# A two-layer encoder step on one core: weights of the feed-forward's first units two units ahead in the program, and leftover output blocks in the last projection

## The chip, the cores and the metric

The kernel runs on one core of a Trainium2 chip. The core has a matrix engine (PE), a vector engine (DVE), a scalar engine (ACT) and a general engine (POOL), each with an instruction queue of its own that runs in order, and a queue (SP) that only starts transfers. Transfers between the chip's memory and the core's on-chip memory run on 16 DMA engines. The metric is the device time of one execution, in microseconds, from the first to the last thing that the core does; lower is better.

## The reference

Two layers work on 640 columns: 512 frames of a new stream and 8 running streams of 16 frames. Each layer has a mixer (layer 0) or an attention (layer 1), and behind it a feed-forward part with a causal convolution of width 3 over the up-projected rows:

```
def _conv_ffn(x, prev, w_up, conv_w, w_down):
    z, st = _causal_dwconv(x @ w_up, conv_w, prev)
    gate, up = jnp.split(z, 2, axis=-1)
    return (jax.nn.silu(gate) * up) @ w_down, st
...
        yp, st_p = _conv_ffn(hp, zero_f, w_up[layer], conv_ffn[layer], w_down[layer])
        ys, st_s = _conv_ffn(hs, state_ffn[layer], w_up[layer], conv_ffn[layer], w_down[layer])
        xp = xp + yp
        xs = xs + ys
```

The model width is 1024 (8 blocks of 128) and the inner width is 2816 (22 blocks of 128 for the gate and 22 for the up rows). All is float32. The change touches only the feed-forward part, which is called once in each layer (`Core.ffn`).

## The kernel before

**Numbers as two halves.** Each float32 operand is held as a high part (a rounded copy, `whi` or `sh` or `hh`) and a low part (the rest, `wlo` or `sl` or `hl`), and each product is three matmuls: high by high, high by low, low by high. A matmul has 320 columns, so 640 columns take two.

There are three ways to make the parts of a weight tile of 128x1024 that SP has loaded into a `raw` buffer. `weights` casts on ACT (L94) and subtracts on DVE (L95). `weights_added` casts on ACT (L102), writes the negative of the high part on ACT (L103) and then lets POOL start a second transfer of the same weights that adds into it (L104); this spares DVE. `weights_down` does the same for two blocks of the down projection (L120, L121, L122).

**Feed-forward.** The 22 units (a block of the gate and the block of the up rows that belongs to it) are grouped in parts of 4, 4, 4, 4, 4 and 2 units (`PARTS`). The first four units are *full units*: 8 chunks times 3 products times 2 halves times 2 blocks, 96 matmuls. Their results are taken out of PSUM by `pad_evac` (DVE, L340 and L341), scaled by the norm's `rb`, which is made beside unit 0 from the PE's column sums and copied out of PSUM on ACT (L325, L326). Then come, for every unit, the convolution `conv` (ACT L346, DVE L348 four times), the gate's silu (L495), the product (L498, L499) and a split into high and low parts.

The other 18 are *pair units*. They compute gate and up rows together with 7 products of 12 matmuls each (`pair_blocks`, `product`, L201) instead of 8. For this the activations are recombined once: `forms` (DVE L152 to L159, behind units 0 and 1) and `settle` (ACT L135 and DVE L136), which overwrites the tiles that the full units read and so must wait for the last of unit 3's matmuls on each of them. The weights are recombined for every unit by `pair_weights`: set A (x11, x12) is the gate tile itself, D (x22) half of the up tile, B (s3, s1) and C (s2, s4) are made by additions (L180) in `raw`, and each set is split (ACT L135, DVE L136). PE uses them in the order A, B, C, B, D, C.

**Down projection.** While the units of one part run, the down projection of the part before is computed, two output blocks in each unit (`downs`, 48 matmuls, between the products of `pair_blocks`), and each block is added to the residual `x` (L359). Parts have 4 units, so 8 output blocks fit. The last part has only 2 units: four output blocks of the part before it (blocks 4 to 7) are left over and are done behind its units, one pair of blocks after the other. At the end `project` does the last part's own down projection for all 8 blocks, 2 chunks each, adds each to `x`, and calls the finish: in layer 0 the next norm's `prep` (ACT L281 and L288, DVE L282, POOL L289), in layer 1 the output's transfer. The last block of layer 1 is done in two halves (`last_block`).

**Buffers.** Weight sets share 5 pairs of buffers `whi` and `wlo`, used in turn in the order in which the program asks for them; `raw` has 4. PSUM has two `zx` buffers and one `d` for blocks, and two `aux`. The order of instructions on each engine is not that of the code: a scheduler, which simulates the program, sets it within what the buffers allow.

**Lead of the weights.** Unit j asks for unit j+1's weights after its own matmuls. Units 0 and 1 use `weights`, units 2 and 3 `weights_added`. For the first pair unit `pair_weights` is called in two pieces (it is a generator with two `yield`s): A before `settle`, the rest behind it. In the later pair units A comes first, then the down weights, then B and C.

## Time and profile before

| | us |
|---|---|
| median of 3 timed runs (1525.31 to 1528.93) | 1527.41 |
| the profiled execution, device time | 1525.84 |
| its span in the profile | 1524.0 |
| feed-forward of layer 0, first evacuation to last | 228.7 to 668 |
| feed-forward of layer 1, first evacuation to the end | 1075.2 to 1524 |

In the profile's rows a start is given in microseconds from the start of the span, then the duration, the engine, the line of the kernel, the operation and its tiles, and in brackets how long the engine had been idle before it and what it had waited for. "xN" joins N alike rows. A busy time of a window counts overlapping instructions of one engine once.

### The profile page before, as it was taken

The page shows a single profiled execution, that of the slowest core. Times are in us where ns is not written, and L with a number is a line of the kernel's source. Part 1 is how long each engine was busy: PE and PEld are TensorE (multiplying, and loading weights), DVE is VectorE, ACT ScalarE, POOL GpSimd, SP SyncE. Part 2 cuts the span into 40 slices and gives each one's busy share as a digit, 9 for nine tenths or more (in the row PEclk, how much of TensorE's full clock was granted, in tenths as well). Part 3 has the DMA queues.
Part 4 walks back from the last instruction along what each step waited for, and adds up shares of the span by engine and source line. Part 5 has one row for each costly group of instructions (what it writes and reads, how often), then busy time and mean ns, then how long its engine had stood idle before and what let it go on. Part 6 is the DMA issues. An engine that isn't in the chain of part 4 may idle for free.

```text
span 1524.0 us, 26325 instructions
## 1 busy us (share of the span) xinstructions
PE 1471.2 (97%) x10576; PEld 1418.3 (93%) x10576; DVE 1047.9 (69%) x1805; ACT 736.9 (48%) x1326; POOL 211.1 (14%) x235
## 2 busy tenths in 40 slices
PE   8999997899999999999999999999699999999998
PEld 6999997899999999989988888888699999999998
DVE  6555438777877777586666657668777686868764
ACT  5422325555555555445544445435455555545551
POOL 4100121101010101135101111003111010101010
PEclk9999998999999999999999999999899999999999
DMA  7222203444444444453534333432254454545342
GB/s 269 77 76 67 67 29 82 133 112 115 106 117 101 115 108 114 81 171 130 171 111 145 109 110 103 161 105 73 54 144 98 99 127 99 127 98 127 97 103 81
DMA packets 74249, 168.04 MB, mean 110 GB/s; under 512 B 13760, under 2 KB 22896, under 8 KB 74000
## 3 DMA queue, kind: packets, MB, share of 16 engines
q1 hardware_dynamic: 49392, 133.79, 27.9%
q0 software_dynamic: 12032, 25.17, 10.4%
q10 hardware_dynamic: 12704, 7.41, 1.6%
q8 instruction: 83, 1.36, 0.4%
q14 instruction: 38, 0.31, 0.1%
HBM read 150.58 MB, written 11.54 MB: 106 GB/s over the span
## 4 chain that ended last, share of the span: by engine, by line
PE 90%; DVE 3%; issue 2%; DMA 2%; ACT 2%; SPq 0%; POOL 0%; DVEq 0%; POOLq 0%
PE mm L251 37%; PE zx L201 20%; PE pj L696 11%; PE aux L201 8%; PE pv L772 3%; PE po L251 2%; PE pt L765 1%; DVE hl L282 1%; PE mm L389 1%; DVE wlo L95 1%; DMA wlo<-w_up 1%; PE pt L851 1%; PE sc L758 1%; PE sc L759 1%; PE scs L830 1%
## 5 line engine op out<-in xcount | busy, mean ns | idle before, releaser
L135 ACT CAST sh<-raw 128x1024 fp32r<-128x1024 f32 (+2 forms) x152 | 142.4, 943 | 192.3 <-PE zx L201 105.4
L251 PE MATMUL mm<-sh,wlo 128*128 128x320 f32 x872 | 203.5, 310 | 5.9 <-ACT sn L216 3.1
L251 PE MATMUL mm<-sh,whi 128*128 128x320 f32 x872 | 200.9, 310 | 2.7 <-ACT sh L135 1.7
L251 PE MATMUL mm<-sl,whi 128*128 128x320 f32 x872 | 199.1, 309 | 0.6 <-DVE sl L136 0.6
L136 DVE TENSOR_TENSOR sl<-raw,sh 128x1024 fp32r<-128x1024 f32 (+2 forms) x152 | 165.0, 1091 | 45.2 <-ACT sh L135 31.0
L348 DVE SCALAR_TENSOR_TENSOR t<-zp,cst,t 128x656 f32<-128x656 f32 x184 | 163.6, 896 | 29.1 <-ACT t L346 28.5
L201 PE MATMUL zx<-hh,sh 128*128 128x320 f32 x576 | 178.2, 309 | 2.0 <-ACT sh L135 1.3
L201 PE MATMUL zx<-hl,sh 128*128 128x320 f32 x576 | 177.8, 309 | 0.0
L201 PE MATMUL zx<-hh,sl 128*128 128x320 f32 x576 | 177.6, 308 | 0.0
L251 PEld LDWEIGHTS mm<-sh,wlo 128*128 128x128 f32 x872 | 147.5, 189 | 6.4 <-ACT sn L216 3.3
L94 ACT CAST whi<-raw 128x1024 fp32r<-128x1024 f32 (+3 forms) x94 | 80.1, 856 | 149.6 <-PE mm L251 85.8
L251 PEld LDWEIGHTS mm<-sh,whi 128*128 128x128 f32 x872 | 146.3, 188 | 4.6 <-ACT sh L135 2.4
L251 PEld LDWEIGHTS mm<-sl,whi 128*128 128x128 f32 x872 | 146.1, 188 | 1.1 <-DVE sl L136 1.1
L696 PE MATMUL pj<-whi,hl 128*128 128x256 f32 x480 | 137.3, 287 | 3.1 <-DVE hl L282 3.1
L359 DVE TENSOR_TENSOR x<-mm,x 128x640 f32<-128x640 f32 x111 | 91.2, 822 | 69.3 <-PE mm L251 69.0
L696 PE MATMUL pj<-wlo,hh 128*128 128x256 f32 x480 | 137.2, 286 | 0.0
L696 PE MATMUL pj<-whi,hh 128*128 128x256 f32 x480 | 136.7, 287 | 0.0
L251 PE MATMUL mm<-hh,whi 128*128 128x320 f32 x512 | 120.3, 317 | 10.4 <-ACT whi L102 10.4
L251 PE MATMUL mm<-hh,wlo 128*128 128x320 f32 x512 | 118.5, 314 | 10.9 <-DMA wlo<-w_up 10.9
L251 PE MATMUL mm<-hl,whi 128*128 128x320 f32 x512 | 119.4, 315 | 2.0 <-DVE hl L282 2.0
L95 DVE TENSOR_TENSOR wlo<-raw,whi 128x1024 fp32r<-128x1024 f32 (+3 forms) x94 | 101.6, 1084 | 23.5 <-ACT whi L94 23.3
L201 PEld LDWEIGHTS zx<-hh,sh 128*128 128x128 f32 x576 | 108.5, 188 | 2.8 <-ACT sh L135 1.5
(232 smaller groups left out, 3350.5 us busy)
## 6 DMA issues: line engine op xcount, KB each, us to landing
raw<-w_up SPq DMA_DIRECT2D x88, 512.0 KB
raw<-w_dn SPq DMA_DIRECT2D x40, 512.0 KB
wlo<-w_dn POOLq DMA_DIRECT2D x40, 512.0 KB, 5.9
raw<-w_c SPq DMA_DIRECT2D x24, 512.0 KB
raw<-w_ab SPq DMA_DIRECT2D x16, 512.0 KB
ck<-c_k SPq DMA_DIRECT2D x16, 512.0 KB
cv<-c_v SPq DMA_DIRECT2D x16, 512.0 KB
o_kv<-z ACTq DMA_DIRECT2D x8, 640.0 KB
```

Of the source, the lines that this page charges most:

```text
L94: nc.scalar.copy(out=hi[:, c], in_=raw[:, c])
L95: nc.vector.tensor_tensor(out=lo[:, c], in0=raw[:, c], in1=hi[:, c].bitcast(F32), op=ALU.subtract)
L135: nc.scalar.copy(out=hi, in_=src)
L136: nc.vector.tensor_tensor(out=lo, in0=src, in1=hi.bitcast(F32), op=ALU.subtract)
L201: nc.tensor.matmul(out, lhsT=l[:, c], rhs=r, start=start and p == 0 and i == 0, stop=p == 3 and i == 2, skip_group_check=True)
L251: nc.tensor.matmul(outs[h], lhsT=l, rhs=r[:, h * HT:(h + 1) * HT], start=start and k == 0, stop=stop and k == 2)
L282: nc.vector.scalar_tensor_tensor(out=lo, in0=x, scalar=gs, in1=hi.bitcast(F32), op0=ALU.mult, op1=ALU.subtract)
L348: nc.vector.scalar_tensor_tensor(out=cv[:, 0:CW], in0=zp[:, i:i + CW], scalar=w[:, i:i + 1], in1=cv[:, 0:CW], op0=ALU.mult, op1=ALU.add)
L359: self.nc.vector.tensor_tensor(out=x, in0=ps[:, C0:C0 + T], in1=x, op=ALU.add)
L389: nc.tensor.matmul(pvs[tb], lhsT=l[:, tb * P:(tb + 1) * P], rhs=r[:, (kc % 2) * 512:(kc % 2 + 1) * 512], start=kc == 0 and k == 0, stop=kc ...
L696: nc.tensor.matmul(out[tb], lhsT=l[:, tb * P:(tb + 1) * P], rhs=r[:, c:c + 256], start=kc == 0 and i == 0, stop=kc == 7 and i == 2)
L772: nc.tensor.matmul(ov[64 * hh:64 * hh + 64, i * P:n], lhsT=z[2][:, j, (2 * pair + hh) * 64:(2 * pair + hh) * 64 + 64], rhs=u[:, j * P:(j + ...
```

## The change

Four things change, all in the feed-forward.

1. The weights of full units 0 and 1 are asked for at the start, and unit j asks for those of unit j+2. The gate set of unit 2 is now made by `weights` (subtraction on DVE) instead of `weights_added`.
2. The whole set of the first pair unit (A, D, B and C) is asked for in unit 2, behind unit 2's matmuls, and no longer around `settle` in unit 3. The down weights of that unit are asked for in unit 3.
3. In the later pair units all of A, B and C comes ahead of the down weights; before, the down weights came between A and B.
4. The four output blocks that were left over (4 to 7, of units 16 to 19) are no longer computed apart: `project` computes them with the last part's two chunks in one sum of 6 chunks, with weight sets of 768 columns made by `weights`. The order of blocks is (4,5), 0, 6, 1, 2, 3, 7, and the next norm's sum of squares starts with block 4 (`first`).

```
@@ -179,7 +179,6 @@
         (g1, g2), (u1, u2) = ((t[:, 0:H], t[:, H:2 * H]) for t in (g, u))
         add = lambda out, a, b: nc.vector.tensor_tensor(out=out, in0=a, in1=b, op=ALU.add)
         A = self.split(self.wp, w, g, 1024)
-        yield
         D = self.split(self.fd, ("dh", "dl"), u2, H)
         add(u2, u1, u2)
         add(u1, u1, g1)
@@ -188,7 +187,7 @@
         add(g2, g2, g1)
         C = self.split(self.wp, w, g, 1024)
         pick = lambda t, i: (t[0][:, i * H:(i + 1) * H], t[1][:, i * H:(i + 1) * H])
-        yield dict(x11=pick(A, 0), x12=pick(A, 1), s3=pick(B, 0), s1=pick(B, 1), s2=pick(C, 0), s4=pick(C, 1), x22=D)
+        return dict(x11=pick(A, 0), x12=pick(A, 1), s3=pick(B, 0), s1=pick(B, 1), s2=pick(C, 0), s4=pick(C, 1), x22=D)
 
     def product(self, out, w, f, name, start):
 
@@ -273,7 +272,7 @@
         return ps
 
 
-    def prep(self, c, x, g, acc, pool, tags, defer=None):
+    def prep(self, c, x, g, acc, pool, tags, defer=None, first=0):
         nc = self.nc
         gs = self.gv[:, 8 * g + c:8 * g + c + 1]
         hi = pool.tile([P, T], F32R, tag=tags[0], name=self.nm("hh"))
@@ -281,7 +280,7 @@
         nc.scalar.activation(out=hi, in_=x, func=AF.Copy, scale=gs)
         nc.vector.scalar_tensor_tensor(out=lo, in0=x, scalar=gs, in1=hi.bitcast(F32), op0=ALU.mult, op1=ALU.subtract)
         def squares():
-            if c == 0:
+            if c == first:
                 nc.scalar.activation(out=acc, in_=x, func=AF.Square)
             else:
                 sq = self.tmp()
@@ -451,14 +450,17 @@
                 y[g] = self.split(rpool, rtags, u[:, :T])
             self.project(io["w_oab"], y, [4, 5, 6, 7, 0, 1, 2, 3], x, finish)
 
-    def project(self, w, acts, order, x, finish, cols=1024, out=None):
-
-        for obs in ((0, 1), (2,), (3,), (4,), (5,), (6,), (7,)):
-            if out is not None and obs == (7,):
-                self.last_block(self.weights(w[7], cols), acts, x[7], out)
+    def project(self, w, acts, order, x, finish, cols=(1024,) * 8, out=None,
+                obs=((0, 1), (2,), (3,), (4,), (5,), (6,), (7,))):
+
+        for group in obs:
+            n = cols[group[0]]
+            mine = acts[len(acts) - n // P:]
+            if out is not None and group == (7,):
+                self.last_block(self.weights(w[7], n), mine, x[7], out)
                 break
-            ps = self.blocks([self.weights(w[ob], cols) for ob in obs], acts, order)
-            for ob, p_ in zip(obs, ps):
+            ps = self.blocks([self.weights(w[ob], n) for ob in group], mine, order)
+            for ob, p_ in zip(group, ps):
                 self.add_x(x[ob], p_)
                 if finish is not None:
                     finish(ob)
@@ -516,9 +518,10 @@
         hk = [h[c] for c in KORD]
         first = [KORD.index(c) for c in range(NC)]
         zi = 0
-        full = lambda j: [(self.weights if j < 2 else self.weights_added)(io["w_up"][l, i]) for i in (j, NJ + j)]
+        full = lambda j: [(self.weights if j < 2 or i == 2 else self.weights_added)(io["w_up"][l, i]) for i in (j, NJ + j)]
         part = lambda j: self.pair_weights(io["w_up"][l, j], io["w_up"][l, NJ + j])
-        w = full(0)
+
+        ahead = [full(0), full(1)]
         for n, (a, b) in enumerate(PARTS):
             si = self.fx.tile([P, 2, 64], F32, tag="si", name=self.nm("si"), bufs=2)
             so = self.fx.tile([P, 2, 72], F32, tag="so", name=self.nm("so"), bufs=2)
@@ -529,36 +532,38 @@
                 zi += 2
                 sts = [si[:, i, 16 * (j - a):16 * (j - a) + 16] for i in range(2)]
                 if j < NSTD:
+                    w = ahead.pop(0)
                     ps = self.blocks(w, hk, first) if j == 0 else [self.blocks([v], hk)[0] for v in w]
-
-                    w = full(j + 1) if j + 1 < NSTD else part(j + 1)
-                    if j + 1 == NSTD:
-                        next(w)
+                    if j + 2 < NSTD:
+                        ahead.append(full(j + 2))
+                    elif j + 2 == NSTD:
+                        ahead.append(part(j + 2))
+                    else:
+                        dn = downs(n, acts, 0)
                         f = [self.settle(p, (h[2 * p], h[2 * p + 1]), forms[p]) for p in range(4)]
                     for z, p_, st in zip((zg, zu), ps, sts):
                         self.pad_evac(z, p_[:, C0:C0 + T], rb, st)
-                    if j + 1 == NSTD:
-                        w = next(w)
                 else:
                     if j == NSTD:
-                        dn = downs(n - 1, prev, left.pop(0))
+                        w = ahead.pop(0)
+                        left.pop(0)
                     else:
                         w = part(j)
-                        next(w)
                         dn = downs(n - 1, prev, left.pop(0))
-                        w = next(w)
                     self.pair_blocks(w, f, zg, zu, sts, dn)
                 for i, z in enumerate((zg, zu)):
                     self.new_state(z, so[:, i, 18 * (j - a):18 * (j - a) + 18])
                 acts.append(act(zg, zu, j))
                 if j < 2:
                     forms += [self.forms(p, x, g, rb, ring, fb) for p in (2 * j, 2 * j + 1)]
-            for ob in left:
-                for d in downs(n - 1, prev, ob):
-                    d()
             nc.scalar.dma_start(out=two(io["o_sf"][l], NB)[:, :, 18 * a:18 * b], in_=so[:, :, 0:18 * (b - a)])
-            prev = acts
-        self.project([io["w_dn"][l, ob][:, a * P:b * P] for ob in range(8)], prev, None, x, finish, cols=(b - a) * P, out=out)
+            if n + 1 < len(PARTS):
+                prev = acts
+
+        a0 = PARTS[-2][0]
+        self.project([io["w_dn"][l, ob][:, (a if ob < left[0] else a0) * P:b * P] for ob in range(8)], prev + acts, None, x, finish,
+                     cols=[(b - (a if ob < left[0] else a0)) * P for ob in range(8)], out=out,
+                     obs=((4, 5), (0,), (6,), (1,), (2,), (3,), (7,)))
 
 
 class Attention:
@@ -917,9 +922,9 @@
 
     h2 = {}
     def fin2(c):
-        if c == 0:
-            fin2.acc = newacc()
-        h2[c] = k.prep(c, x[c], 2, fin2.acc, k.hp, HT_)
+        if not h2:
+            fin2.acc, fin2.first = newacc(), c
+        h2[c] = k.prep(c, x[c], 2, fin2.acc, k.hp, HT_, first=fin2.first)
         if c < 6:
             nc.sync.dma_start(out=io["s_x"][c], in_=x[c])
     k.ffn(0, x, done(h1), 1, rb, ring, fb, fin2)
```

ACT (layer 0, around the convolution of unit 1), before: the casts of unit 2's two sets (`whi_2278`, `whi_2285`) and their negatives. The L352 copies and L346 are the evacuation's followers in unit 1.

```order
L352 COPY so_2016<-zp_90 128x18
L102 CAST whi_2278<-raw_2276 128x1024
L352 COPY so_2016<-zp_88 128x18
L346 ACTIVATE t_2298<-zp_88,cst 128x656
L346 ACTIVATE t_2302<-zp_90,cst 128x656
L135 CAST sh_2161<-raw_2156 128x960
L103 ACTIVATE wlo_2279<-whi_2278 128x1024
L135 CAST sh_2174<-raw_2169 128x960
L102 CAST whi_2285<-raw_2283 128x1024
L103 ACTIVATE wlo_2286<-whi_2285 128x1024
```

ACT, the same place with the change: `whi_2136` is unit 2's up set, `rb` the norm's scale, L351 and L345 (here of unit 0) the same lines as L352 and L346 before.

```order
L324 COPY rb_1974<-aux_1981 128x512
L325 COPY rb_1974<-aux_1982 128x128
L528 DMA si_2027<-st_f 128x2x64
L528 DMA si_2645<-st_f 128x2x64
L102 CAST whi_2136<-raw_2134 128x1024
L351 COPY so_2028<-zp_88 128x18
L103 ACTIVATE wlo_2137<-whi_2136 128x1024
L351 COPY so_2028<-zp_89 128x18
L345 ACTIVATE t_2149<-zp_89,cst 128x656
L345 ACTIVATE t_2153<-zp_88,cst 128x656
L497 ACT_TABLE_LOAD
L497 ACTIVATE t_2153<-t_2153 128x656
```

The cast and the negative of unit 2's up set now stand right behind `rb`, ahead of unit 0's convolution; before, both of unit 2's sets stood in unit 1's convolution. Unit 3's (`whi_2291`, `whi_2298`) now stand where unit 2's stood.

DVE (layer 0, end of unit 3), before: `sl_2611` and `sl_2617` are the low parts of B and C of the first pair unit, `hl` the low parts that `settle` writes, L180 the additions for B and C, L340 and L341 evacuations.

```order
L136 TENSOR_TENSOR sl_2611<-raw_2575,sh_2610 128x1024
L180 TENSOR_TENSOR raw_2574<-raw_2574 128x512
L498 TENSOR_TENSOR t_2469<-t_2464,t_2460 128x512
L499 TENSOR_TENSOR t_2469<-t_2464,t_2460 128x128
L340 TENSOR_TENSOR zp_88<-mm_2476,rb_1974 128x512
L341 TENSOR_TENSOR zp_88<-mm_2476,rb_1974 128x8x16
L136 TENSOR_TENSOR hl_1574<-y_2152,hh_1573 128x640
L136 TENSOR_TENSOR sl_2617<-raw_2574,sh_2616 128x1024
L136 TENSOR_TENSOR hl_1643<-y_2165,hh_1642 128x640
L136 TENSOR_TENSOR sl_2473<-t_2469,sh_2472 128x640
```

DVE, the same place with the change: `sl_2466` is the low part of B, and L339 and L340 are the evacuation of unit 3's up block.

```order
L339 TENSOR_TENSOR zp_89<-mm_2548,rb_1974 128x512
L136 TENSOR_TENSOR hl_1580<-y_2166,hh_1579 128x640
L340 TENSOR_TENSOR zp_89<-mm_2548,rb_1974 128x8x16
L180 TENSOR_TENSOR raw_2452<-raw_2452,raw_2451 128x512
L136 TENSOR_TENSOR hl_1706<-y_2179,hh_1705 128x640
L136 TENSOR_TENSOR hl_1832<-y_2328,hh_1831 128x640
L136 TENSOR_TENSOR hl_1958<-y_2341,hh_1957 128x640
L136 TENSOR_TENSOR sl_2496<-t_2492,sh_2495 128x640
L180 TENSOR_TENSOR raw_2451<-raw_2452,raw_2451 128x512
L347 SCALAR_TENSOR_TENSOR t_2628<-zp_89,cst,t_2628 128x656
L347 SCALAR_TENSOR_TENSOR t_2632<-zp_88,cst,t_2632 128x656
L136 TENSOR_TENSOR sl_2466<-raw_2452,sh_2465 128x1024
```

The low part of B moved from ahead of the eight `hl` of `settle` to behind them all, behind the product of unit 3 and behind two of its convolution steps.

ACT (layer 1, the end of the projection ahead of the feed-forward), before: `whi_11868` and `whi_11874` are the sets of unit 1.

```order
L281 ACTIVATE hh_11644<-x_79,gv 128x640
L288 ACTIVATE t_11648<-x_79 128x640
L281 ACTIVATE hh_11683<-x_80,gv 128x640
L288 ACTIVATE t_11687<-x_80 128x640
L281 ACTIVATE hh_11722<-x_81,gv 128x640
L288 ACTIVATE t_11726<-x_81 128x640
L325 COPY rb_11738<-aux_11745 128x512
L326 COPY rb_11738<-aux_11746 128x128
```

ACT, the same place with the change: `whi_11857` is unit 2's gate set, `whi_11864` its up set.

```order
L94 CAST whi_11857<-raw_11856 128x1024
L280 ACTIVATE hh_11699<-x_81,gv 128x640
L287 ACTIVATE t_11703<-x_81 128x640
L102 CAST whi_11864<-raw_11862 128x1024
L103 ACTIVATE wlo_11865<-whi_11864 128x1024
L324 COPY rb_11715<-aux_11722 128x512
L325 COPY rb_11715<-aux_11723 128x128
L351 COPY so_11756<-zp_11422 128x18
```

Here the cast and the negative of unit 2's up set stand ahead of `rb`, and that cast takes the buffer of unit 0's gate set.

ACT (a pair unit), before: `sh_3024` is A of the unit, `whi_3029` and `wlo_3030` its down weights; its B (`sh_3041`) comes later.

```order
L135 CAST sh_2846<-raw_2819 128x1024
L135 CAST sh_3024<-raw_3020 128x1024
L120 CAST whi_3029<-raw_3028 128x1024
L238 COPY zp_90<-zx_2649 128x192
L239 COPY zp_90<-zx_2649 128x8x16
L121 ACTIVATE wlo_3030<-whi_3029 128x1024
```

ACT, with the change: `sh_3033` and `sh_3039` are B and C of the same unit, `whi_3044` and `wlo_3045` its down weights.

```order
L135 CAST sh_3039<-raw_3019 128x1024
L215 ACTIVATE sn_3066<-zx_3050 128x320
L351 COPY so_2646<-zp_90 128x18
L345 ACTIVATE t_3003<-zp_90,cst 128x656
L120 CAST whi_3044<-raw_3043 128x1024
L121 ACTIVATE wlo_3045<-whi_3044 128x1024
L135 CAST sh_3224<-raw_3220 128x1024
```

The down weights moved from behind A to behind C in the order in which the five buffers are taken.

60 lines of the change are left out of this document (32 added, 28 removed).

## Prediction

> **What bounds the kernel now.** The table of windows comes first, cut at the borders of the feed-forward's stages. Its columns are the window, its length, the busy time of PE, its weight loads, DVE, ACT and POOL with the instructions behind each, the granted clock, the DMA share and GB/s.
>
> ```profile
> span 1524.0 us, 26325 instructions
> ...
> 243.40:284.00 40.60, 31.52 (x194) 30.86 (x193) 32.86 (x51) 22.75 (x30) 8.21 (x8) 0.83 0.56 145
> 284.00:307.00 23.00, 17.62 (x102) 16.14 (x101) 16.72 (x26) 13.15 (x22) 3.90 (x4) 0.93 0.41 98
> 307.00:640.00 333.00, 333.00 (x2274) 333.00 (x2273) 248.34 (x359) 179.53 (x291) 34.29 (x51) 1.00 0.45 110
> 1088.50:1131.00 42.50, 30.34 (x178) 29.29 (x177) 31.85 (x51) 22.20 (x29) 7.32 (x8) 0.80 0.58 138
> 1131.00:1155.00 24.00, 19.62 (x118) 18.41 (x117) 18.05 (x28) 14.31 (x24) 3.88 (x4) 0.93 0.41 96
> 1155.00:1483.00 328.00, 328.00 (x2240) 328.00 (x2239) 245.00 (x354) 178.43 (x289) 34.32 (x51) 1.00 0.46 110
> ```
>
> From 307 to 640 and from 1155 to 1483 PE never stops: 333.00 us for 2274 matmuls, 0.1465 us each. Nothing can be gained there, only lost. The two stretches ahead of them are the entries, full units 2 and 3 and the first pair units. Their 296 matmuls (194 + 102, and 178 + 118) would take 43.4 us in each layer; they take 40.60 + 23.00 = 63.6 and 42.50 + 24.00 = 66.5. So layer 0 loses 20.2 us and layer 1 loses 23.1. The waits of PE (engine and line, what it waited for, total us, times, longest) say for what:
>
> ```profile
> PE mm L251 <- DMA wlo<-w_up: 10.9, 2, 8.0
> PE mm L251 <- ACT whi L102: 10.4, 3, 6.2
> ...
> PE mm L251 <- DMA wlo<-w_dn: 2.8, 1, 2.8
> PE mm L251 <- DVE hl L282: 2.0, 1, 2.0
> ...
> PE mm L477 <- DVE x L359: 1.0, 1, 1.0
> PE mm L251 <- DVE x L359: 0.9, 1, 0.9
> ...
> PE mm L477 <- DVE x L478: 0.6, 1, 0.6
> ```
>
> 21.3 us of waits are for the weights of full units. The timelines of ACT, of POOL and of PE in layer 0 show how they come late:
>
> ```profile
> 244.93 0.21 ACT L352 COPY so<-zp 128x18 f32<-128x18 f32 x1 [6.28 <-DVE zp L341]
> ...
> 247.40 1.05 ACT L103 ACTIVATE wlo<-whi 128x1024 fp32r<-128x1024 f32 x1
> 249.24 1.04 ACT L102 CAST whi<-raw 128x1024 fp32r<-128x1024 f32 x1
> ```
>
> ```profile
> 248.79 1.07 POOL L104 DMA_DIRECT2D wlo<-w_up  x1 [13.68 <-DVE t L348]
> ```
>
> ```profile
> 250.33 0.90 PE L251 MATMUL mm<-hh,whi 128*128 128x320 f32 x2 [6.18 <-ACT whi L102]
> 254.66 0.90 PE L251 MATMUL mm<-hh,wlo 128*128 128x320 f32 x2 [2.90 <-DMA wlo<-w_up]
> 255.36 0.73 PE L251 MATMUL mm<-hh,whi 128*128 128x320 f32 x2
> 255.89 0.73 PE L251 MATMUL mm<-hl,whi 128*128 128x320 f32 x2
> ...
> 260.25 0.46 PE L251 MATMUL mm<-hl,whi 128*128 128x320 f32 x2
> 260.55 0.46 PE L251 MATMUL mm<-hh,wlo 128*128 128x320 f32 x2
> ...
> 293.07 0.55 PE L251 MATMUL mm<-sh,wlo 128*128 128x320 f32 x2 [2.81 <-DMA wlo<-w_dn]
> ```
>
> ACT had been idle for 6.28 us in front of unit 1's L352, with unit 2's weights queued behind it; the accumulation started at 248.79 and PE's wait for it ended at 254.66. After such a wait PE runs at half speed for a while: a pair of matmuls steps 0.53 us (255.36 to 255.89) and later 0.30 (260.25 to 260.55). A stretch of some 3.4 us so costs about 1.5 us more.
>
> The wait of 2.81 us at 293.07 was also followed by half speed (granted clock 0.93 in its window). [...]
>
> **The change part by part.** The sum is made against the profiled execution's 1525.84 us; the median of the runs is 1.57 us above it.
>
> *Units 2 and 3.* Unit 2's casts leave unit 1's convolution; ahead of it nothing is missing. Unit 3's now stand where unit 2's stood, so by the rows above its first low set lands at about 255 to 257; it is needed at 257.5. PE then runs units 2 and 3 from 243.40 without a wait: 192 x 0.1465 = 28.1, to 271.5, against 284.0.
>
> *What is late next: DVE.* PE's next work, the first pair unit, needs X and Z (24 matmuls, with settle's eight low parts) and then B. Only 4 of B's matmuls can go without its low part: 28 x 0.1465 = 4.1, so PE stands at 275.6. On DVE this low part now comes behind all of settle. How long DVE takes to it follows from the trace of before, with the window from the first evacuation to 293.02 (DVE only), the groups by form, and DVE's timeline:
>
> ```profile
> 228.70:293.02 64.32, 54.23 (x86) 0.89 0.47 119
> ```
>
> ```profile
> L136 DVE TENSOR_TENSOR sl<-raw,sh 128x1024 fp32r<-128x1024 f32 x4 | 4.9, 1221 | 0.2
> ...
> L180 DVE TENSOR_TENSOR raw<-raw 128x512 f32<-128x512 f32 x3 | 2.1, 687 | 0.0
> ```
>
> ```profile
> 228.72 0.69 DVE L340 TENSOR_TENSOR zp<-mm,rb 128x512 f32<-128x512 f32 x1 [4.78 <-PE mm L251]
> ...
> 231.43 3.34 DVE L348 SCALAR_TENSOR_TENSOR t<-zp,cst,t 128x656 f32<-128x656 f32 x4 [1.02 <-ACT t L346]
> 235.59 0.69 DVE L498 TENSOR_TENSOR t<-t,t 128x512 f32<-128x512 f32 x1 [0.82 <-ACT t L495]
> ```
>
> By the order of instructions the same work stands ahead of B's low part with the change, less three additions, one 128x512 and two 128x1024 low parts, plus two convolution steps. Neighbours overlap by 0.085 us, so that is 54.23 - 4 x 0.60 - 2 x 1.14 + 2 x 0.82 = 51.2. With the two early waits, 1.02 + 0.82, it ends at 228.72 + 51.2 + 1.8 = 281.7. PE waits 281.7 - 275.6 = 6.1 us, in one piece or split between Z's low parts and B. Add 1.5 for one half-speed stretch, and 2 (between 0 and 4) for C's low part and the first down set, which come right behind. Layer 0 then loses 9.6 of its 20.2: **-10.6**.
>
> *Layer 1* has the same chain with one difference: unit 2's up cast, which needs unit 0's gate buffer, and its negative stand ahead of `rb` on ACT, and DVE's first evacuation waits for `rb`.
>
> ```profile
> 1074.53 0.59 ACT L325 COPY rb<-aux 128x512 f32<-128x512 f32 x1 [8.99 <-PE aux L324]
> ```
>
> ```profile
> 1059.93 2.58 DVE L95 TENSOR_TENSOR wlo<-raw,whi 128x1024 fp32r<-128x1024 f32 x1
> ```
>
> Unit 1 begins one unit (14.1 us) ahead of 1088.5, at 1074.4, and the gate's last matmul of unit 0 is six matmuls earlier, at about 1073.5: there the buffer comes free; two ACT operations of 1.05 later `rb` starts at about 1075.7, 1.2 to 1.4 late. DVE starts at 1075.15 + 1.35 and ends B's low part at 1076.5 + 53.0 = 1129.5. PE comes there from 1088.5 + 28.1 + 4.1 = 1120.7, plus 0.8 (next term): it waits 8.0. With 1.5 and 2 the loss is 11.5 of 23.1: **-11.6**.
>
> *Lead-in of layer 1.* Unit 2's gate set needs a DVE subtraction more ahead of the feed-forward, where PE already waits 2.0 us for DVE (`hl` L282). Between 1.1 and the 2.58 us of the row above, of which one part is hidden: **+0.8** (0 to 2.6). In layer 0 ACT and DVE have slack there: 0.
>
> *End.* The blocks behind the last product are now four or six chunks long, and the first two of 6 chunks (72 matmuls, 10.5 us) cover the last convolution. Of the three waits 1.0 + 0.9 + 0.6 I take **-2.3**. Layer 0's own end changes by less than 1 either way: 0. The eight additions to `x` saved are on DVE, off PE's path.
>
> *Pair units.* This is the cost. A down set now takes the buffer of a later set. By the order of instructions 104 to 144 matmuls stand before between the matmul that frees the buffer and the first that reads the new low part; with the change 57 to 60 in 15 of 34 sets, 63 to 67 in 13, 77 to 84 in 6. What must fit between, from the timelines of PE, ACT and POOL and from the transfers of `wlo`:
>
> ```profile
> 337.86 0.31 PE L201 MATMUL zx<-hh,sl 128*128 128x320 f32 x1
> ```
>
> ```profile
> 338.06 1.05 ACT L120 CAST whi<-raw 128x1024 fp32r<-128x1024 f32 x1 [0.41 <-PE zx L201]
> 339.15 1.06 ACT L121 ACTIVATE wlo<-whi 128x1024 fp32r<-128x1024 f32 x1
> ```
>
> ```profile
> 340.64 1.22 POOL L122 DMA_DIRECT2D wlo<-w_dn  x1 [3.45 <-ACT wlo L121]
> ```
>
> ```profile
> wlo<-w_up POOLq DMA_DIRECT2D x8, 512.0 KB, 8.3
> ```
>
> ```profile
> DMA to landing us min/median/max: 5.7/5.9/6.7
> ```
>
> 340.64 - 337.86 + 5.9 = 8.7 us. Before, 104 matmuls gave 15.2, so nothing showed. Now 57 to 60 give 8.4 to 8.8, 63 to 67 give 9.2 to 9.8. 15 sets a little late, about 0.15 each: **+2.5** (0 to 15, below).
>
> Sum: -10.6 - 11.6 + 0.8 - 2.3 + 2.5 = -21.2, so 1504.6 profiled, **1506** as a median.
>
> **Rivals.**
>
> *The down sets come late everywhere.* The last row above has a maximum of 6.7; with that the chain is 9.5, 15 sets are late by 0.9 and 13 by about 0.15: 15.5 us instead of 2.5, and 1519. For it: the accumulation now starts nearer to the two `raw` loads of the next unit. Against it: the median in these units is 5.9. Chance 0.15.
>
> *Slower than before.* The same place, with the price of the accumulations of `w_up`, median 8.3, which ran beside other loads. The chain is then 11.1; 15 sets late by 2.5 and 13 by 1.6 cost 58 us: about 1562. It decides from 0.8 us of lateness per set on average (34 x 0.8 = 27: the 24 gained elsewhere and 3 more). Against it: the loads are as many as before in each unit, at a DMA share of 0.45. Chance 0.06. [...]
>
> *DVE doesn't bind.* If the low parts come in time, the entries lose nothing: -20.2 - 23.1 - 2.3 + 0.8 + 2.5 = -42, 1485. The count of DVE's work speaks against it. Chance 0.04.
>
> *The change doesn't do what it says.* Unit 3's low parts are late as unit 2's were, because they take the same place in ACT's queue. Landing 10 us after POOL's start they would hold PE 3 us and a half-speed stretch in each layer, part of which DVE's wait hides: 1510 to 1516. Chance 0.07.
>
> **How the numbers follow.** Forecast 0.68, the rivals 0.15, 0.06, 0.04 and 0.07. The range 1496 to 1520 takes in late down sets and, at the low end, a DVE wait smaller by 5 us in each layer; it leaves out the slower case, the case without DVE's bound, and some of each tail. Runs of this kernel can tell about 0.2%, 3 us. Faster: nearly all of forecast, late sets, no bound and half-done, 0.89. Slower 0.06, same 0.05.
>
> **What would show it.** Right: units 2 and 3 without a wait in both layers; PE's longest wait at L200 on DVE `hl` or `sl` of 3 to 8 us, at about 275 to 282; the first waits for `wlo<-w_dn` between 307 and 640, each under half a microsecond. Wrong: waits for `wlo<-w_dn` of over a microsecond in most pair units (the rival), a PE that waits for `whi` L102 again, or no DVE wait at all.

## The result, and the profile after

The changed kernel takes 1505.37 us (median of 4 runs, 1503.4 to 1505.42), the kernel before 1527.44 (4 runs, 1525.31 to 1528.93). The ratio is 0.9853, with a 95% interval of 0.9836 to 0.987. The profiled execution took 1503.4 us, 22.4 less than that of before, in the spans too.

The windows of the changed kernel come first, cut at the same stages as those of before (the columns are the same: window, length, PE, weight loads, DVE, ACT, POOL, clock, DMA share, GB/s).

```profile
span 1501.6 us, 26356 instructions
```

```profile
243.40:271.60 28.20, 28.20 (x194) 28.20 (x194) 27.75 (x45) 18.01 (x27) 5.62 (x6) 1.00 0.35 80
271.60:295.00 23.40, 18.52 (x95) 16.93 (x94) 22.58 (x35) 13.90 (x21) 6.30 (x3) 0.78 0.51 138
295.00:620.00 325.00, 324.64 (x2206) 323.14 (x2205) 241.79 (x345) 172.82 (x285) 30.50 (x49) 1.00 0.45 110
1070.00:1120.00 50.00, 43.45 (x269) 41.12 (x268) 48.90 (x79) 26.95 (x40) 7.05 (x8) 0.91 0.31 77
1120.00:1145.00 25.00, 24.95 (x157) 24.55 (x157) 19.73 (x28) 14.54 (x23) 2.83 (x4) 0.91 0.59 148
1145.00:1462.00 317.00, 314.20 (x2136) 312.93 (x2135) 232.49 (x334) 166.38 (x272) 27.37 (x47) 1.00 0.43 107
1462.00:1502.00 40.00, 35.83 (x243) 35.29 (x241) 17.26 (x26) 7.08 (x14) 0.00 (x0) 1.00 0.23 81
```

Units 2 and 3 now run in 28.20 us where before they took 40.60: PE is busy throughout. The loss has moved behind them. In 271.60 to 295.00 the 95 matmuls would take 13.9 us at 0.1465; they take 23.4, so 9.5 are lost, at a granted clock of 0.78, while DVE is busy for 22.58 of 23.40. And the pair units, which lost nothing before, lose a little: in layer 1 2136 matmuls would take 312.9 us and take 317.0.

The waits of PE in the whole span say for what (engine and line, what it waited for, total us, times, longest):

```profile
PE aux L200 <- DVE sl L136: 5.3, 2, 2.7
...
PE mm L250 <- DMA wlo<-w_dn: 2.6, 4, 1.0
PE zx L200 <- DVE hl L136: 2.0, 4, 0.8
PE mm L250 <- DVE hl L281: 2.0, 1, 2.0
PE zx L200 <- ACT sn L215: 1.9, 2, 1.3
PE zx L200 <- ACT sh L135: 1.7, 1, 1.7
...
PE mm L479 <- DVE x L480: 0.6, 1, 0.6
...
PE mm L250 <- DMA wlo<-w_up: 0.4, 1, 0.4
```

The 21.3 us of waits for the weights of full units are down to 0.4. At the entries PE now waits for DVE (L136, the low parts of B and of `settle`) and for ACT (L215 and L135). The four waits for down weights lie in the pair units, one in layer 0 and three in layer 1, 1.0 us at most.

Where the 22.4 us went is read by taking the n-th matmul of the program in both traces (each holds 10,576) and the difference of its start. The stages are cut at the matmuls that start at 243.4, 320, 640, 1074.3, 1170 and 1483 in the kernel before; the first difference is 0. "Middle" runs from the pair units of layer 0 through its end and the attention to unit 1 of layer 1.

| stage | forecast, us | measured, us |
|---|---|---|
| entry of layer 0 | -10.6 | -11.0 |
| pair units of layer 0 and of layer 1 | +2.5 | +2.0 and +4.2 |
| middle | +0.8 | -3.8 |
| entry of layer 1 | -11.6 | -10.7 |
| end | -2.3 | -3.0 |
| all | -21.2 | -22.4 |

Two terms were off, by 3.7 (pair units) and by 4.6 (middle), and they offset each other. That the sum came within 1.2 us of the measured change is luck in that part.

### The profile page after: what moved, and what is told of

Its sections match the earlier page's. It is cut to its first block, busy times and chain, and to the rows that moved or that the text cites. A ratio compares the mean times of both kernels' runs of the same rounds, so it can differ in the third digit from the quotient of the medians.

```text
span 1501.6 us, 26356 instructions
## 1 busy us (share of the span) xinstructions
PE 1470.4 (98%) x10576; PEld 1417.9 (94%) x10576; DVE 1050.5 (70%) x1799; ACT 727.0 (48%) x1316; POOL 194.5 (13%) x229
## 4 chain that ended last, share of the span: by engine, by line
PE 88%; DVE 6%; DMA 2%; ACT 2%; issue 2%; SPq 0%; ACTq 0%; DVEq 0%
PE mm L250 36%; PE zx L200 19%; PE pj L701 12%; PE aux L200 8%; PE pv L777 3%; PE po L250 3%; DMA wlo<-w_dn 2%; PE pt L770 1%; DVE hl L281 1%; DVE wlo L95 1%; PE mm L388 1%; PE pt L856 1%; PE sc L763 1%; PE sc L764 1%; DVE sl L136 1%
## 5 line engine op out<-in xcount | busy, mean ns | idle before, releaser
L135 ACT CAST sh<-raw 128x1024 fp32r<-128x1024 f32 (+2 forms) x152 | 142.8, 943 | 135.7 <-PE zx L200 87.0
L136 DVE TENSOR_TENSOR sl<-raw,sh 128x1024 fp32r<-128x1024 f32 (+2 forms) x152 | 165.0, 1092 | 55.4 <-ACT sh L135 55.2
L250 PE MATMUL mm<-sh,wlo 128*128 128x320 f32 x864 | 197.8, 310 | 3.2 <-DMA wlo<-w_dn 2.6
L250 PE MATMUL mm<-sh,whi 128*128 128x320 f32 x864 | 196.6, 310 | 0.6 <-ACT sh L135 0.6
L94 ACT CAST whi<-raw 128x1024 fp32r<-128x1024 f32 (+3 forms) x96 | 85.8, 896 | 148.9 <-PE mm L250 81.6
L250 PEld LDWEIGHTS mm<-sh,wlo 128*128 128x128 f32 x864 | 143.6, 188 | 5.9 <-DMA wlo<-w_dn 2.8
L358 DVE TENSOR_TENSOR x<-mm,x 128x640 f32<-128x640 f32 x103 | 84.5, 820 | 90.7 <-PE mm L250 90.4
L95 DVE TENSOR_TENSOR wlo<-raw,whi 128x1024 fp32r<-128x1024 f32 (+3 forms) x96 | 107.9, 1127 | 34.3 <-ACT whi L94 33.7
L200 PEld LDWEIGHTS zx<-hl,sh 128*128 128x128 f32 x576 | 108.4, 188 | 4.1 <-DVE hl L136 3.9
```

What stands on the lines that cost most here:

```text
L94: nc.scalar.copy(out=hi[:, c], in_=raw[:, c])
L95: nc.vector.tensor_tensor(out=lo[:, c], in0=raw[:, c], in1=hi[:, c].bitcast(F32), op=ALU.subtract)
L135: nc.scalar.copy(out=hi, in_=src)
L136: nc.vector.tensor_tensor(out=lo, in0=src, in1=hi.bitcast(F32), op=ALU.subtract)
L200: nc.tensor.matmul(out, lhsT=l[:, c], rhs=r, start=start and p == 0 and i == 0, stop=p == 3 and i == 2, skip_group_check=True)
L250: nc.tensor.matmul(outs[h], lhsT=l, rhs=r[:, h * HT:(h + 1) * HT], start=start and k == 0, stop=stop and k == 2)
```

## The experiments

Each is set against runs of the kernel before on the same chip. The stages of all of them, cut as above (differences to the kernel before in us, one profiled execution each; "start" is all that lies ahead of unit 2 in layer 0, which none of the edits is meant to move):

| | start | entry 0 | pairs 0 | middle | entry 1 | pairs 1 | end | span |
|---|---|---|---|---|---|---|---|---|
| the change | 0.0 | -11.0 | 2.0 | -3.8 | -10.7 | 4.2 | -3.0 | -22.4 |
| ring_back | 0.7 | -7.9 | 0.1 | -3.8 | -10.0 | 0.0 | -3.0 | -23.8 |
| ring_only | -0.3 | -1.0 | 2.9 | 2.5 | 0.1 | 9.8 | 0.6 | 14.6 |
| merge_only | -0.4 | 0.6 | 0.0 | -3.9 | 0.9 | 0.0 | -3.0 | -5.8 |
| lead_only | -0.1 | -7.9 | 0.1 | 0.4 | -10.4 | 0.0 | 0.0 | -18.0 |
| ring_late | 1.9 | -10.9 | 0.1 | -3.7 | -10.7 | 0.0 | -3.0 | -26.2 |
| pool_adds | 1.0 | -12.7 | 2.6 | -3.4 | -15.0 | 4.5 | -3.0 | -26.0 |
| more_dve | -0.4 | -7.3 | 1.2 | -5.1 | -11.1 | 6.4 | -3.0 | -19.3 |
| late_added | 1.5 | -6.7 | 0.0 | -5.4 | -14.1 | 0.0 | -3.0 | -27.6 |
| added_dn | 0.1 | -11.6 | 0.0 | -5.4 | -13.6 | 0.0 | -3.0 | -33.4 |

### The order of the buffers alone, undone and done

*ring_back* is the changed kernel with the down weights of every pair unit but the first between A and B again:

```
         A = self.split(self.wp, w, g, 1024)
+        yield
...
-        return dict(x11=...
+        yield dict(x11=...
...
-                        ahead.append(part(j + 2))
+                        ahead.append(list(part(j + 2))[-1])
...
                         w = part(j)
+                        next(w)
                         dn = downs(n - 1, prev, left.pop(0))
+                        w = next(w)
```

> The changed kernel, but in the pair units the down weights are asked for between A and B again, as before; everything else of the change stays. Theory (the down sets take a buffer that comes free too late): 96 to 174 matmuls stand again between the matmul that frees the buffer and the first use, so all waits for wlo<-w_dn in the pair units go, and with them the 6 us that both stretches of pair units lost (1.7 in layer 0, 4.2 in layer 1): about 1499.5 us, PE busy without a gap in both stretches. Rival (the waits are due to transfers that collide, whichever buffer is taken): landings and waits stay, about 1505 us. The entries stay as they are with the change in both theories (about 10 and 13 us lost).

Measured: 1501.15 us (1499.01 to 1501.95, 4 runs), ratio 0.9824 (0.9809 to 0.9839), 4.2 us under the change by the medians. Its windows:

```profile
271.60:300.00 28.40, 21.50 (x112) 19.45 (x111) 25.39 (x38) 17.21 (x27) 7.52 (x4) 0.85 0.57 152
300.00:640.00 340.00, 340.00 (x2317) 340.00 (x2316) 251.30 (x360) 178.77 (x293) 34.64 (x49) 1.00 0.43 106
1150.00:1462.00 312.00, 312.00 (x2130) 312.00 (x2130) 233.90 (x336) 166.07 (x271) 30.09 (x46) 1.00 0.44 107
```

The pair units are full again, 340.00 of 340.00 and 312.00 of 312.00. So the order of the buffers costs what the pair units lose, about 6 us. Late landings alone cost nothing: two sets of layer 0 landed after 7.5 and 7.0 us in this run, and PE did not wait. But the entry of layer 0, which was expected to stay as it is, gets 3.1 us worse, and PE's timeline shows the new wait there:

```profile
297.36 0.56 PE L251 MATMUL mm<-sh,wlo 128*128 128x320 f32 x2 [2.12 <-DMA wlo<-w_dn]
```

These are the first pair unit's down weights, whose place no edit moved. SP's load of weights for a later unit comes sooner beside them, in the timelines of POOL and SP of ring_back and then of the changed kernel:

```profile
290.21 1.22 POOL L122 DMA_DIRECT2D wlo<-w_dn  x1
290.57 0.33 SPq L177 DMA_DIRECT2D raw<-w_up  x1
```

```profile
289.51 1.22 POOL L122 DMA_DIRECT2D wlo<-w_dn  x1
293.46 0.33 SPq L177 DMA_DIRECT2D raw<-w_up  x1
```

In ring_back ACT's cast of the second pair unit's down weights, which frees a `raw` buffer, ended at 290.54, just ahead of the load. With the load 0.36 us behind it the set landed after 7.11 us, with the load 3.95 us behind it after 5.77. That the load is what made it late is likely (lead_only below has 0.38 and 7.07, ring_late 3.50 and 5.89), but no run separated it. The new order is better at this place, and worse everywhere else.

*ring_only* is the kernel before with the new order of buffers and nothing else (there, too, the first pair unit keeps the order of before):

```
                         w = part(j)
                         next(w)
-                        dn = downs(n - 1, prev, left.pop(0))
                         w = next(w)
+                        dn = downs(n - 1, prev, left.pop(0))
```

> The kernel before, with one part of the change: in the pair units A, B and C are asked for ahead of the down weights. Theory (late buffer): the pair units lose some 4 to 6 us in all, 1531 to 1533 us, with waits for wlo<-w_dn of up to 1 us each in both layers. Rival (the waits come from the lead's transfers): no change, 1527 us. Entries and ends as before.

Measured: 1531.96 us (1529.17 to 1540.41, 10 runs) beside 1527.27 (19 runs), ratio 1.004 (1.0022 to 1.0058): 4.7 us slower by the medians. The profiled run was the slowest of the ten, so its row in the table is that of a bad run. Its waits, and the landings of the low parts between 1155 and 1483:

```profile
PE mm L251 <- DMA wlo<-w_dn: 11.3, 10, 2.7
```

```profile
DMA to landing us min/median/max: 5.7/6.5/8.3
```

The same line of the kernel before, and then of the changed kernel between 1145 and 1462:

```profile
DMA to landing us min/median/max: 5.7/5.8/6.6
```

```profile
DMA to landing us min/median/max: 5.7/5.9/7.3
```

The price of the order depends on the landing times of the run. In the changed kernel four sets of layer 1 landed 6.85 to 7.25 us after their start; three of them held PE up by 0.9 to 1.3 us each, the fourth by nothing. The others, at 5.7 to 6.6, cost 0 to 0.4. In this run of ring_only they came later, and ten waits made 11.3 us. Why they land late in one run and not in another is not settled; the runs of ring_only spread over 11.2 us, those of before over 6.6.

### The merged output blocks alone, and the lead alone

*merge_only* is the kernel before with `project`, `prep` and the last lines of `ffn` as in the change (part 4 of it):

```
-            for ob in left:
-                for d in downs(n - 1, prev, ob):
-                    d()
...
+        self.project([io["w_dn"][l, ob][:, (a if ob < left[0] else a0) * P:b * P] for ob in range(8)], prev + acts, None, x, finish,
+                     cols=[(b - (a if ob < left[0] else a0)) * P for ob in range(8)], out=out,
+                     obs=((4, 5), (0,), (6,), (1,), (2,), (3,), (7,)))
```

> The kernel before, with one part of the change: the four left-over output blocks join the last part's projection. Theory: it alone gives what the ends gave, about 4 us at the end of layer 0 (up to the first matmul of the attention's output) and 2.7 us at the end of layer 1: about 1520.7 us; entries and pair units as before. Rival (the 4 us at the end of layer 0 follow from the lead, not from the merge): about 1524.7 us.

Measured: 1522.06 us (1518.64 to 1525.67, 10 runs), ratio 0.9963 (0.9951 to 0.9974). 3.0 us of it lie at the end, as forecast. The rest lies in the middle. The next windows hold layer 0's last matmuls and the attention, up to the matmuls that follow it; PE's work in them is the same but for nine matmuls, which the two with the merge have more (before, changed kernel, merge_only; PE's busy time follows the length):

```profile
663.20:1033.50 370.30, 364.55 (x3199) 324.98 (x3198) 254.86 (x666) 180.60 (x429) 65.66 (x61) 1.00 0.40 126
```

```profile
653.80:1019.90 366.10, 362.93 (x3208) 325.23 (x3206) 251.64 (x666) 176.66 (x426) 55.68 (x62) 1.00 0.41 128
```

```profile
663.00:1029.10 366.10, 362.95 (x3207) 325.31 (x3205) 251.68 (x666) 176.69 (x426) 55.23 (x59) 1.00 0.41 128
```

This stretch, whose attention no edit touched, is 4.2 us shorter with the merge, with the lead in the program or without it. PE stands in it for 3.2 us instead of 5.8: three waits of before (1.2, 0.7 and 0.4 us, for `sh`, `sl` and `up`) are gone. The scheduler orders it anew: by the names of the tiles, PE's matmuls in the attention stand in one and the same order in all eight kernels with the merge, and 2613 of 3122 places differ from the order before. In lead_only, which has no merge, no place differs. So the merge brings the new order; whether by the order of the output blocks or by their longer sums, no run separated.

*lead_only* is ring_back without the merge, so the kernel before with parts 1 and 2 of the change.

> The kernel before with the lead alone: weights of full units two units ahead and the first pair unit's set in unit 2, without the merge and with the down weights between A and B in the later pair units. If the parts add up (ring_back is lead and merge, 1501.2; the merge alone gave 5.2): 1506.4 us, entries as ring_back, ends as before, no loss in the pair units. If the lead needs the merge or the new order for its gain: over 1510 us.

Measured: 1508.78 us (1507.84 to 1510.68, 4 runs), ratio 0.9871 (0.9856 to 0.9886); 18.0 us less in the profile. Its entries are those of ring_back (-7.9 and -10.4 beside -7.9 and -10.0), and middle and end are near those of before. The parts add up: -18.0 and merge_only's -5.8 make -23.8, which is ring_back's. To the tenth this is luck: in lead_only the attention, in the order of before, was 1.1 us shorter than before, so single traces differ by about that much.

### Both orders where each is better

*ring_late* is ring_back, but the second pair unit (j = 5) has its down weights behind C:

```
                         next(w)
-                        dn = downs(n - 1, prev, left.pop(0))
-                        w = next(w)
+                        if j == NSTD + 1:
+                            w = next(w)
+                            dn = downs(n - 1, prev, left.pop(0))
+                        else:
+                            dn = downs(n - 1, prev, left.pop(0))
+                            w = next(w)
```

> As ring_back (down weights between A and B again), but the second pair unit keeps the order of the change. ring_back lost 4 us more than the change in layer 0's entry (a wait of 2.1 us for wlo<-w_dn at 297.4) and none behind it. Theory: that loss comes from the order in the second pair unit alone; here the entry loses 10 us in layer 0 as with the change, the units behind it lose nothing: some 4 us better than ring_back in layer 0 and up to 1 in layer 1, 1496 to 1498 us. Rival (the entry's loss moves to the next unit whatever the order): 1500 to 1501 us.

Measured: 1498.89 us (1495.55 to 1500.3, 4 runs), ratio 0.9802 (0.9771 to 0.9833). The entry of layer 0 is back at -10.9, the pair units lose 0.1. That settles the account of the buffers' order: the new one is worth 3 us at one unit of layer 0 and costs 6 us in the others.

### Does DVE set the entries?

Three kernels take work from DVE there or add to it. For these, PE's waits and its time at half speed in the two entries (us; half speed is a granted clock of 0.5 in the trace; the entries are cut as above):

| | entry 0: waits | half speed | entry 1: waits | half speed |
|---|---|---|---|---|
| the change | 4.8 | 10.2 | 6.5 | 13.7 |
| ring_late | 5.4 | 10.2 | 6.7 | 13.7 |
| pool_adds | 4.4 | 3.4 | 5.1 | 3.4 |
| more_dve | 8.9 | 6.8 | 7.4 | 6.8 |
| late_added | 7.8 | 10.2 | 6.0 | 3.4 |
| added_dn | 5.4 | 6.8 | 5.4 | 10.2 |

Half speed changes from kernel to kernel by more than the waits do. So what an entry gains or loses does not by itself say whether DVE set it; the waits say it better.

*pool_adds* is the changed kernel with the four additions of the first pair unit's weights on POOL:

```
-    part = lambda j: self.pair_weights(io["w_up"][l, j], io["w_up"][l, NJ + j])
+    part = lambda j: self.pair_weights(io["w_up"][l, j], io["w_up"][l, NJ + j], nc.gpsimd if j == NSTD else None)
```

> The changed kernel, but the four additions for sets B and C of the first pair unit run on POOL instead of DVE, in both layers. Theory (DVE bounds the entry): by the new order B's low part comes three additions, one low part and two convolution steps earlier on DVE, 4.2 us, and C's too; PE's waits of 5 to 7 us in each entry shrink by 3 to 4 us, and the half-speed stretch may go: 1494 to 1499 us. Rival 1 (POOL and DVE slow each other, as the subtraction of 2.58 us beside a POOL addition): DVE operations beside the POOL additions take twice as long, and little is gained: 1503 to 1505 us. Rival 2 (PE's waits there are set by ACT or by transfers): no change, 1505 us.

Measured: 1504.37 us (1499.84 to 1505.93, 4 runs), ratio 0.9842 (0.9823 to 0.9862). That is 1.0 us under the change by the medians, where the first rival had put it. The profiled run was the fastest of the four, 4.5 us under their median; in it the entries gain 1.7 and 4.3 us over the change. The timelines of POOL and of DVE show why the waits hardly shrink:

```profile
269.60 4.05 POOL L181 TENSOR_TENSOR raw<-raw,raw 128x512 f32<-128x512 f32 x2
```

```profile
269.51 1.14 DVE L136 TENSOR_TENSOR sl<-raw,sh 128x960 fp32r<-128x960 f32 x1
270.58 1.92 DVE L136 TENSOR_TENSOR hl<-y,hh 128x640 fp32r<-128x640 f32 x1
272.42 2.25 DVE L136 TENSOR_TENSOR sl<-raw,sh 128x960 fp32r<-128x960 f32 x1
```

In the changed kernel, where POOL does not add, `hl` and `sl` of these sizes take 0.81 and 1.15 us. So the two at 270.58 and 272.42, which DVE started while an addition ran on POOL, took 1.11 and 1.10 us longer, more than the 0.68 that the addition took on DVE itself; the one at 269.51, which had started 0.09 us ahead of POOL's addition, lost nothing. By the table above PE's waits shrink by 0.4 and 1.4 us only. The rest of the gain goes with the clock, 3.4 us at half speed in each entry for 10.2 and 13.7.

*more_dve* is the changed kernel with one pair's two `hl` subtractions in `settle` done twice (the second writes the same numbers):

```
             self.part(hi, lo, y)
+            if p == 0:
+                self.nc.vector.tensor_tensor(out=lo, in0=y, in1=hi.bitcast(F32), op=ALU.subtract)
```

> The changed kernel with two DVE subtractions of 0.74 us more in settle of each layer (two low parts are written twice with the same values). Theory (DVE bounds the entry): B's low part comes 1.5 us later in each layer and PE's waits for DVE grow by as much: 1505.4 + 3 = 1508.4 us, in the profile 1.2 to 1.8 us more lost in each entry. Rival (something else, ACT or a transfer, sets the end of PE's waits): 1505 us, no change.

Measured: 1507.05 us (1506.48 to 1509.57, 4 runs), ratio 0.9864 (0.9839 to 0.9889), 1.7 above the change by the medians, which is within both intervals. B's low part starts at 282.37 instead of 281.25, and with a start 0.4 earlier it is 1.5 us later, as the added work is long. The entry of layer 0 is 3.7 us worse, where 1.2 to 1.8 were expected. In layer 1 the added work cost nothing (-11.1 for -10.7): PE's waits grew by 0.9 us there too, but it ran 6.8 us at half speed in place of 13.7. The waits grow in both layers, as they must if DVE sets them, but a microsecond of DVE is not a microsecond of PE.

*late_added* is ring_late, with the low parts of A and D of the first pair unit made as those of unit 3 are, by a negative on ACT and an accumulating transfer, not by DVE:

```
-        A = self.split(self.wp, w, g, 1024)
+        A = self.added(self.wp, w, g, gate, 1024, 1024) if lows else self.split(self.wp, w, g, 1024)
         yield
-        D = self.split(self.fd, ("dh", "dl"), u2, H)
+        D = self.added(self.fd, ("dh", "dl"), u2, up[:, H:2 * H], H, H) if lows else self.split(self.fd, ("dh", "dl"), u2, H)
```

> As ring_late, and in the first pair unit of each layer the low parts of sets A and D (weights as they are, not sums) are made by ACT and an accumulating transfer instead of a DVE subtraction. Theory (DVE bounds the entry): DVE has 1.7 us less ahead of B's low part, and in the new order the product's low part and two convolution steps (2.4 us) stand behind it: 4 us sooner in each layer, unlike POOL additions without slowing DVE. Entries 4 to 6 us shorter in each layer than ring_late: 1486 to 1490 us. Rival 1 (the new low part of A lands late, 8 to 10 us after POOL's start, as those of unit 3 did): a wait for wlo<-w_up of 1 to 3 us at the first product instead, 1490 to 1494 us. Rival 2 (DVE does not bind): no gain over ring_late.

Measured: 1498.02 us (1496.27 to 1498.18, 4 runs), ratio 0.9799 (0.9776 to 0.9823): 0.9 us under ring_late, far from what was expected. Layer 1's entry gained 3.4 us, 0.7 of it in waits and the rest with the clock (3.4 us at half speed for 13.7). Layer 0's lost 4.2, and PE's timeline has the reason:

```profile
295.48 0.87 PE L251 MATMUL mm<-sh,wlo 128*128 128x320 f32 x2 [4.44 <-DMA wlo<-w_dn]
296.15 0.73 PE L251 MATMUL mm<-sh,whi 128*128 128x320 f32 x2
```

With DVE out of the way PE gets to the first set of down weights earlier than that lands, waits 4.4 us for it, and runs at half speed behind the wait, to about 301.6 (a pair of matmuls steps 0.53 us there, and 0.29 behind it).

### The version that is faster than both

*added_dn* is late_added, with the first pair unit's down weights asked for in unit 2, between A and D, and no longer in unit 3:

```
-                        ahead.append(list(part(j + 2))[-1])
+                        w2 = part(j + 2)
+                        next(w2)
+                        dn = downs(n, acts, 0)
+                        ahead.append(next(w2))
                     else:
-                        dn = downs(n, acts, 0)
```

> As late_added, but the down weights of the first pair unit are asked for in unit 2, between sets A and D, instead of in unit 3. late_added took DVE's wait away and PE then waited 4.4 us in layer 0 (at 295.5, then at half speed) and 2.6 us in layer 1 for the low part of exactly these weights, whose cast stood on ACT behind set C. Theory (what is late next is this cast): their low part lands some 8 to 10 us sooner, the wait goes, and the entries are 4 to 7 us shorter in layer 0 and 2 to 4 in layer 1 than in late_added: 1488 to 1492 us. Rival (C's low part, which comes one place later on DVE, takes over): 1495 to 1498 us, PE waiting for DVE at L201.

Measured: 1492.9 us (1489.81 to 1493.99, 4 runs) beside 1527.92 (7 runs), ratio 0.9762 (0.9744 to 0.9781). Its windows:

```profile
243.50:271.50 28.00, 28.00 (x193) 28.00 (x192) 27.42 (x47) 19.33 (x29) 5.64 (x8) 1.00 0.55 122
271.50:295.00 23.50, 18.07 (x99) 17.22 (x98) 18.22 (x28) 12.56 (x21) 3.92 (x3) 0.85 0.42 119
295.00:620.00 325.00, 325.00 (x2220) 325.00 (x2219) 246.24 (x354) 177.18 (x288) 32.88 (x50) 1.00 0.45 111
1135.00:1450.00 315.00, 315.00 (x2152) 315.00 (x2151) 235.99 (x340) 169.35 (x275) 30.07 (x48) 1.00 0.45 109
```

The pair units are full in both layers. In the entry of layer 0 DVE is down from 22.58 us (changed kernel, nearly the same window) to 18.22, and in neither layer is it what PE waits for. Layer 0's entry gains 4.9 us over late_added, as expected. Layer 1's, expected to gain 2 to 4, is 0.5 us longer: its waits are 0.6 us shorter, but 10.2 us are at half speed in place of 3.4. The largest waits that are left in the entries:

```profile
PE zx L201 <- ACT sn L216: 4.8, 2, 3.4
PE mm L251 <- DMA wlo<-w_dn: 3.6, 2, 3.0
```

So the entry has a chain of limits close behind each other: weights of full units, DVE, the first down set, ACT's evacuation `sn`. Each that is taken away shows the next one.

## Why the prediction was right, point by point

**Units 2 and 3 without a wait: right, with little room.** Layer 0 has none. Unit 3's first low set was forecast to land at 255 to 257 and to be needed at 257.5. POOL started it at 250.24 and it landed 7.40 us later, at 257.64, behind the forecast stretch; PE's first matmul that reads it is this one:

```profile
258.04 0.46 PE L250 MATMUL mm<-hh,wlo 128*128 128x320 f32 x2
```

It had 0.4 us to spare; in layer 1 PE waited for such a set, 0.38 us. The half-done rival, in which unit 3's low parts come late, was only this far away.

**DVE is late next: right.** The forecast put the end of B's low part at 281.7 and PE's wait for it into one piece or two, 6.1 us together. PE's timeline and DVE's:

```profile
275.18 0.41 PE L200 MATMUL zx<-hh,sh 128*128 128x320 f32 x1 [1.34 <-ACT sn L215]
...
276.95 0.41 PE L200 MATMUL zx<-hl,sh 128*128 128x320 f32 x1 [0.82 <-DVE hl L136]
...
277.68 0.58 PE L200 MATMUL zx<-hl,sh 128*128 128x320 f32 x1
278.06 0.47 PE L200 MATMUL zx<-hh,sl 128*128 128x320 f32 x1
278.33 0.47 PE L200 MATMUL zx<-hh,sh 128*128 128x320 f32 x1
...
282.52 0.63 PE L200 MATMUL aux<-sh,sl 128*128 128x320 f32 x1 [2.65 <-DVE sl L136]
```

```profile
281.25 1.22 DVE L136 TENSOR_TENSOR sl<-raw,sh 128x1024 fp32r<-128x1024 f32 x1
282.38 0.68 DVE L180 TENSOR_TENSOR raw<-raw 128x512 f32<-128x512 f32 x1
```

B's low part ended at 282.47, and the waits are 1.34 + 0.82 + 2.65 = 4.8 us. The first of them is for ACT's evacuation `sn`, which stood behind a cast that had itself waited 0.82 us for DVE (L501). The longest, 2.65, stays under the 3 to 8 us that the prediction gave as a sign of being right. The total lost, 9.5, is what was forecast (9.6), but made up otherwise, so the close agreement is luck: the waits are 1.3 shorter, and half speed is longer. It runs from 277.68 to about 287.9 (granted clock 0.50), 10.2 us where the forecast had one stretch of some 3.4; beside the waits 9.5 - 4.8 = 4.7 us are lost where the forecast had 1.5, and 2 for C's low part and the first down set, which cost nothing here. That DVE sets the longest wait is shown by the rows above, where PE starts 0.05 us after B's low part ends, and by more_dve, where the waits grow; late_added shows that the first down set is close behind.

**Layer 1's entry: right in size, with a wrong step.** The forecast had `rb` 1.2 to 1.4 us late, because two operations for unit 2's up set stand ahead of it on ACT, and because unit 0's buffer comes free at the gate's last matmul. The scheduler had let that happen earlier: ACT's cast started at 1059.49, 2.0 us ahead of unit 1's first matmul at 1061.50. DVE's first evacuation starts 0.73 us after unit 1 does, at 1062.23, as it did before (1075.15 against 1074.42). Nothing was late there. What took its place is on DVE, at C:

```profile
1114.67 0.48 DVE L222 TENSOR_TENSOR zp<-zx,sn 128x320 f32<-128x320 f32 x1
1115.07 1.71 DVE L347 SCALAR_TENSOR_TENSOR t<-zp,cst,t 128x656 f32<-128x656 f32 x2
1116.69 0.68 DVE L180 TENSOR_TENSOR raw<-raw 128x512 f32<-128x512 f32 x1
```

In layer 0 the addition for C (L180) follows B's low part at once, at 282.38. Here one evacuation and two convolution steps stand between, 2.0 us, and PE waits 1.74 us more for C's high part, at 1119.58. In all PE's waits in this entry are 6.5 us where 8.0 were forecast, and it runs 13.7 us at half speed where the forecast had one stretch of some 3.4; the two offset each other here too. The working also let the 0.8 us of the lead-in move PE and not DVE, whose evacuations follow PE.

**The middle: missed.** The sum has no term for the attention; the nearest step is "Layer 0's own end changes by less than 1 either way: 0". It was put at nothing without a reason, and the stretch with the attention became 4.2 us shorter, with the merge alone too (merge_only).

**The lead-in of layer 1: the size was near, the cause was wrong.** The forecast charged 0.8 us to one more subtraction on DVE. PE's wait there did not grow: it is 1.98 us before and 2.00 after. What differs is the speed behind it (granted clock 0.50 from 1049.5 to 1052.5 with the change, 1.00 from 1064 to 1067 before), in the timelines of PE of the changed kernel and of the kernel before:

```profile
1048.90 0.69 PE L250 MATMUL mm<-hl,whi 128*128 128x320 f32 x2 [2.00 <-DVE hl L281]
1049.39 0.73 PE L250 MATMUL mm<-hh,wlo 128*128 128x320 f32 x2
```

```profile
1063.37 0.56 PE L251 MATMUL mm<-hl,whi 128*128 128x320 f32 x2 [1.98 <-DVE hl L282]
1063.77 0.45 PE L251 MATMUL mm<-hh,wlo 128*128 128x320 f32 x2
```

That costs 1.5 us: in the table the middle is -3.4 to -3.9 in the kernels with the merge that fell to half speed, and -5.1 to -5.4 in more_dve, late_added and added_dn, which did not. Merge_only has no more subtractions there than the kernel before, waits 1.99 us, and fell to half speed. So the subtraction is not the cause.

**The pair units: the mechanism was right, the size too small.** The term was "15 sets a little late, about 0.15 each: +2.5 (0 to 15)"; it measured 6.2. Most sets did land at 5.7 to 6.1 us as assumed. In layer 0 the one wait for down weights behind 295 is 0.2 us, as forecast; in layer 1 there are three, of 1.0, 0.7 and 0.7. Working with the median left out the few sets that land at about 7: with no slack, three of them held PE up by 3.2 us. The rival "The down sets come late everywhere" is the same mechanism with every set at 6.7. It did not come here, but the slowest run of ring_only, with a median landing of 6.5 in layer 1, lost 12.7 us in the pair units, near that rival's 15.5.

**The end: right.** -3.0 for -2.3, in every kernel with the merge.

## What to carry to other kernels

When a wait is removed, count the work of every engine up to the next thing that the waiting engine needs: here that count told that about half of what the entries lost would stay lost, and each later experiment that removed one limit met the next within a few microseconds. An order of buffers that leaves a transfer no slack was priced here by its late landings (three sets at about 7 us cost 3.2 us in layer 1), not by its median of 5.9; give the slack back where the engine is otherwise full, and use the tight order only where it saves a wait. Where a scheduler orders the program, compare the stages that the change does not touch as well. And read the clock beside the waits before a gain is put down to an engine.

## What the runs showed of the hardware

- **Half speed followed short waits, and not always the same ones.** In the kernel before it lasted 3.4 us (293.75 to 297.13) behind the wait of 2.81 us. In layer 0 of the changed kernel it began at 277.68, after waits of 1.34 and 0.82 us within some 3 us. At the lead-in of layer 1 the same wait of 1.97 to 2.00 us was followed by half speed in the changed kernel, merge_only, lead_only, ring_back, ring_late and pool_adds, and by full speed in the kernel before, ring_only, more_dve, late_added and added_dn. Why the same wait has both outcomes, no run shows.
- **DVE's subtractions that started beside an addition on POOL were slower** in layer 0 of pool_adds: 1.92 and 1.89 us for 0.81, 2.25 for 1.15, and 1.12 for 0.81 where the addition ended 0.44 us after the start; the additions took 1.9 to 2.1 us each. A subtraction that had started 0.09 us earlier than an addition took 1.14.
- **Landings of alike accumulating transfers** (512 KB, in the pair units) took between 5.7 and 8.3 us, with a median in layer 1 of 5.8 in the kernel before, 5.9 with the change and 6.5 in ring_only.
